# A hybrid decoder layer on one core: first norm, state-gate blocks, split heads and last norms reordered

## The chip, the cores and the metric

One core of a Trainium2 chip runs the whole program. Its engines work side by side, each from its own in-order queue: TensorE (PE: matmuls, with weight loads shown apart as PEld), VectorE (DVE), ScalarE (ACT), GpSimd (POOL) and SyncE (SP, which issues DMAs; ACT and POOL can issue DMAs too). An engine stops at an instruction whose semaphore has not come. The metric is the device time of one execution in microseconds (us).

## The reference

```python
xn = rmsnorm(h, norm1_g)                     # h: 16 meta tokens and 512 tokens, 1024 channels
u_s, x_m, z_m, g_s, g_m = split(xn @ w_in)
y_s = s5_branch(u_s, ...) @ w_ssm_out        # diagonal SSM scan, gelu, y * sigmoid(y @ w_glu)
y_m = mlstm_branch(x_m, z_m, ...) @ w_ml_out # conv, silu, gates, 4 heads of matrix memory
mixed = sigmoid(g_s) * y_s + sigmoid(g_m) * y_m
h = h + mixed @ w_out
h = h + peer_ffn(rmsnorm(h, norm2_g), ...)   # top 16 of 16384 one-neuron experts, 8 heads
return rmsnorm(h, final_norm_g)[:, 16:]
```

Everything is float32, and the norms divide by the root of the mean square of a token's 1024 channels.

## The kernel before

Each float32 matmul is done as three fast ones: an operand x is split into a rounded half `x_h` (made on ACT) and the rest `x_l` (made on DVE or POOL, as x minus `x_h`), and `mm3` issues high x high, high x low and low x high. Weights come in blocks of 128x1024: `wblock` loads one over SP's queue and splits it, the low half on POOL for some block numbers. A scheduler sets the order of the instructions on each engine from the order in which the code is written and from its own times; `later`, `behind` and `keep_in_program_order` add constraints. Four tiles (`pmm`) and four more (`ptr`) of PSUM take the products.

The stages, in the order of PE's work:

- **First norm and u.** x comes transposed, in pieces `xr0`, `xr1` (eight blocks k of 128 channels). ACT writes `xnh` = x times the norm's scale `g1` (L246), DVE the rest `xnl` (L247). The root of the mean square (`sqt`, `ssp`, `n1...`, `nt`) is applied behind the products.
- **SSM, conv and state gates.** The SSM's input blocks (`wx0` to `wx7`) give `xm`; DVE drains each half into `xmt` (L181) and runs a causal convolution into `xct` (three steps each, L443), followed by a sigmoid on ACT (L446). State-gate blocks `gs0` to `gs7` (L82, L85, L86; weights `wgs`) stand between them; 24 matmuls each. The scan's output `ys` (copied by ACT at L579) is turned round through DRAM: eight writes `yd` (L586), eight reads `yt` (L588), then gelu into `yg` (L661) and its split `ygh`, `ygl`.
- **Forget and input gates.** `gate` (64 matmuls with the zero-padded weights `wgt`) is copied with a bias into `rwa` (L606) and turned by `xtp`, `lip` and later `lfp`; log-sigmoid and two scans of DVE follow.
- **glu, so, heads.** `glu` and `so` finish the SSM branch. Four heads follow; each ends by writing its two blocks of `xct`. When all are done, the eight blocks are split into `ymh`, `yml` and `mo0` to `mo7` multiply them.
- **wo and q.** `wo` gives h (tiles `x0`, `x12`, `x3q`); for each of four token tiles the second norm makes `xn`, PE transposes it (`x2t`) and it is split into `x2h`, `x2l`; the queries `q0`, `q1` read these, half of the tokens at a time.
- **Experts.** The scores, the choice of experts, hidden products (`h`) and a loop over 128 keys j: `w` and `v` are split and `o0`, `o1`, `o2` collect the products of token tiles 1 to 3; tile 0 is summed by DVE in `ac0`. The last keys' products run tile by tile.
- **Last norm.** For each token tile in turn: two adds into `hr` (L1482), squares on ACT, two multiplications by the final scale (`sq`, L1484), a chain of ten small DVE operations for 1/root, and two scalings and two DMAs out.

Of the kernel before, what the change touches and what calls it, by code (L numbers as in the profile page):

```python
# [126 lines left out]
def front(tc, a, dbg, cst, dram, xnp, ident, h2d, gds, x0, qt01, dump, split, mm3, rsqrt, rsqrt_cols):  # L127
# [3 lines left out]
    with es:  # L131
# [58 lines left out]
        xr = [half(f"xr{j}", f"x{'cm'[j]}t0") for j in range(2)]  # L190
        g1 = small("g1", (P, NK), a["par"][:, :NK])
        wu = [None] * 4
        for k in range(0, NK, 2):
            (SY, A)[k // 2 % 2].dma_start(xr[k // 4][:, k % 4:k % 4 + 2], a["xt"][k // 2])
            if k == 0:
                wu[0] = wblock(a["w_in"][0], "wu0")
        wu[1] = wblock(a["w_in"][1], "wu1")

# [358 lines left out]
        for b, n in ((0, 0), (8, 2)):  # L557
            V.tensor_copy(wgt[:, b:b + 8, :2 * H], wgs[:, n])

# [160 lines left out]
        V.tensor_copy(cb[:, 14:18], cbp[:, 14:18])  # L720
        p5.close()
        pm_ = ExitStack()
        phase["pool"] = pm_.enter_context(tc.tile_pool(name="pmh", bufs=2, reuse_waits="tile"))
        phase["q"] = pm_.enter_context(tc.tile_pool(name="pmq", bufs=12, reuse_waits="tile"))
        zs_ = {}
# [71 lines left out]
        pms, squares = {}, []  # L797

        def weights(h):

            mup = phase["q"].tile([P, S], F32, tag="mu", name=f"mu{h}", bufs=2)
            SY.dma_start(mup, mud[h:h + 1].to_broadcast([P, S]))
# [16 lines left out]
        for h in range(H):  # L819
# [62 lines left out]
        phase["pool"] = es.enter_context(tc.tile_pool(name="pe", bufs=1, reuse_waits="tile"))  # L882
        ymh = [half(f"ymh{j}", f"pA{j}", (P, 4, S), F32R) for j in range(2)]
        yml = [half(f"yml{j}", f"pB{j}", (P, 4, S), F32R) for j in range(2)]
# [35 lines left out]
        g2, ss2 = None, []  # L920
        for c, slots in ((0, ("xct0", "xct1", "mix0", "xmt0")), (1, ("pA0", "pA1", "pB0", "pB1"))):
            wo = wout(c, slots)
            if c == 1:
# [4 lines left out]
                wq = [wblock(a["w_q"][s_], f"wq{s_}") for s_ in range(2)]  # L928
                qp = []
            for i in range(NT):  # L930
                p = pmm(f"wo{i}{c}")
# [13 lines left out]
                if i == 1:  # L945
                    xn12, xn3 = half("xn12", "xct0", (P, 2, D)), half("xn3", "xct1", (P, 2, D))
                xn = (xn12[:, 0], xn12[:, 1], xn3[:, 0])[i - 1] if i else x0
                V.scalar_tensor_tensor(xn, xs[i], rstd, g2, op0=OP.mult, op1=OP.mult)
                for j in range(2):
                    p = ptr(f"x2t{i}{j}", (P, 4, P))  # L950
                    for k in range(4):
                        PE.transpose(p[:, k], xn[:, (4 * j + k) * P:(4 * j + k + 1) * P], ident)
                    split(xh[j][:, :, i * P:(i + 1) * P], xl[j][:, :, i * P:(i + 1) * P], p)

        for t in (slice(0, S // 2), slice(S // 2, S)):
            for s_ in range(2):
                if t.start == 0:
                    qp.append(pmm(f"q{s_}"))
                proj(*wq[s_], qp[s_][:, t], lambda k: [x[k // 4][:, k % 4, t] for x in (xh, xl)])
                A.copy(qt01[:, s_, t], qp[s_][:, t])  # L960
        if dbg is not None and "h2" in dbg:
# [4 lines left out]
def peer(tc, a, out, dbg, cst, dram, xh, xl, blanks, ident, h2d, gds, x0, qt01, dump, split, mm3, rsqrt_cols):  # L966
# [20 lines left out]
    with es:  # L987
# [420 lines left out]
        def products(i, j, wh, wl, vh, vl, pin=None, halves=(0, 1)):  # L1408
# [4 lines left out]
            return last  # L1413

        due = 0
        loop[0] = True
        for j in range(NKEY):
# [23 lines left out]
            for last in (0, 1):  # L1441
# [116 lines left out]
```

## Time and profile before

| | |
|---|---|
| median of 3 runs | 1695.78 us (1695.61 to 1697.59) |
| profiled execution | 1696.09 us, its span 1694.4 us |
| PE / PEld busy | 97% / 86% of the span |
| DVE / ACT / POOL busy | 76% / 41% / 42% |
| mean granted TensorE clock | 0.993 of 2.4 GHz |

The span runs from the first to the last instruction; the time holds 1.7 us more around it. PE is busy nearly throughout, so what can be won lies in the few places where PE stands still, runs at a lower clock, or has not begun or has ended. The page cuts the span into 40 slices of 42 us; the first and the last of them are those with PE at 7 and 6 tenths, all others at 9.

### The profile page before, as it was taken

What the parts mean: (1) busy time and instruction counts of PE and PEld (TensorE: products, weight loads), DVE (VectorE), ACT (ScalarE), POOL (GpSimd) and SP (SyncE); (2) the same over time, 40 slices, a digit from 0 to 9 for tenths busy, and PEclk for the clock granted to TensorE, in tenths of its full rate; (3) what the DMA queues carried; (4) which work ended last, traced back from release to release, by engine and by line L of the source; (5) the groups of instructions that cost most, each with busy time, mean ns of one, the idle gap of its engine ahead of it and who ended that gap; (6) DMA issues with size and microseconds to landing.
All of it is one profiled execution on the core that took longest, in us unless ns stands there. A gap on an engine that the chain in (4) does not pass through costs nothing.

```text
span 1694.4 us, 25464 instructions
## 1 busy us (share of the span) xinstructions
PE 1650.4 (97%) x9387; PEld 1461.3 (86%) x9387; DVE 1279.9 (76%) x2599; ACT 690.6 (41%) x1021; POOL 709.3 (42%) x476
## 2 busy tenths in 40 slices
PE   7999999999999999999999999999999999999996
PEld 6888688777888899999999988888888888888885
DVE  6995642266478899977884598878878897888876
ACT  4543545432332334556664433333333333333323
POOL 2011022223122378888886043333335564554520
PEclk9999999999999999999999999999999999999998
DMA  5514254212452347699999999999998999999963
GB/s 184 119 51 100 63 199 153 70 40 75 173 199 87 112 91 183 155 271 299 297 300 337 350 380 400 337 345 360 350 362 318 363 391 368 362 371 349 335 245 129
DMA packets 173364, 409.83 MB, mean 242 GB/s; under 512 B 44468, under 2 KB 89652, under 8 KB 172088
## 3 DMA queue, kind: packets, MB, share of 16 engines
q1 hardware_dynamic: 113624, 266.51, 45.4%
q0 software_dynamic: 55328, 134.31, 23.3%
q10 hardware_dynamic: 4288, 7.39, 1.3%
q8 instruction: 73, 1.20, 0.3%
q14 instruction: 51, 0.42, 0.1%
HBM read 360.86 MB, written 47.29 MB: 241 GB/s over the span
## 4 chain that ended last, share of the span: by engine, by line
PE 84%; DVE 8%; DMA 4%; ACT 2%; issue 2%; POOL 0%; SPq 0%; ACTq 0%; DVEq 0%; POOLq 0%
PE h L82 10%; PE h L85 10%; PE h L86 10%; PE o L82 10%; PE o L86 10%; PE o L85 10%; PE gp L1333 2%; PE q L86 2%; PE q L85 2%; PE q L82 2%; DMA wo<-in_w_out 1%; PE s L839 1%; PE n L848 1%; PE gm L346 1%; PE gm L349 1%
## 5 line engine op out<-in xcount | busy, mean ns | idle before, releaser
L82 PE MATMUL h<-x2h,uh 128*128 128x384 f32 x1024 | 345.5, 337 | 0.2 <-ACT act L1024 0.2
L85 PE MATMUL h<-x2l,uh 128*128 128x384 f32 x1024 | 343.5, 335 | 0.0
L86 PE MATMUL h<-x2h,ul 128*128 128x384 f32 x1024 | 343.2, 335 | 0.0
L85 PE MATMUL o<-vl,wh 128*128 128x512 f32 x768 | 280.1, 391 | 0.8 <-DVE vl L79 0.8
L82 PE MATMUL o<-vh,wh 128*128 128x512 f32 x768 | 280.3, 391 | 0.2 <-ACT wh L1435 0.2
L1043 POOL DMA_INDIRECT g<-in_v,e x128 | 200.2, 1564 | 187.7 <-DVE ac L1058 169.1
L86 PE MATMUL o<-vh,wl 128*128 128x512 f32 x768 | 266.5, 390 | 0.5 <-DVE wl L1450 0.5
L1267 POOL DMA_INDIRECT gds<-gw,ix x128 | 239.7, 1872 | 46.3 <-issue 36.9
L1043 POOL DMA_INDIRECT g<-in_u,e x103 | 115.6, 1122 | 217.3 <-DVE jk L1050 214.3
L79 DVE TENSOR_TENSOR vl<-v,vh 128x1024 fp32r<-128x1024 f32 x128 | 156.2, 1220 | 63.5 <-ACT vh L78 63.3
L79 DVE TENSOR_TENSOR ul<-u,uh 128x1024 fp32r<-128x1024 f32 x128 | 156.1, 1219 | 56.1 <-ACT uh L78 45.4
L78 ACT ACTIVATE uh<-u 128x1024 fp32r<-128x1024 f32 x128 | 135.4, 1058 | 152.6 <-PE h L85 119.8
L82 PEld LDWEIGHTS h<-x2h,uh 128*128 128x128 f32 x1024 | 192.3, 188 | 4.1 <-ACT act L1024 0.5
L85 PEld LDWEIGHTS h<-x2l,uh 128*128 128x128 f32 x1024 | 192.3, 188 | 1.9
L86 PEld LDWEIGHTS h<-x2h,ul 128*128 128x128 f32 x1024 | 192.3, 188 | 1.8
L78 ACT ACTIVATE vh<-v 128x1024 fp32r<-128x1024 f32 x128 | 134.6, 1055 | 103.3 <-issue 73.0
L86 PEld LDWEIGHTS o<-vh,wl 128*128 128x128 f32 x768 | 144.2, 188 | 31.4 <-DVE wl L1450 1.2
L85 PEld LDWEIGHTS o<-vl,wh 128*128 128x128 f32 x768 | 144.1, 188 | 30.2 <-DVE vl L79 1.1
L82 PEld LDWEIGHTS o<-vh,wh 128*128 128x128 f32 x768 | 143.7, 188 | 27.6 <-ACT wh L1435 0.5
L1058 DVE SCALAR_TENSOR_TENSOR ac<-g,w,ac 128x1024 f32<-128x1024 f32 x127 | 162.4, 1279 | 0.0
L1024 ACT ACTIVATE act<-h 128x384 f32<-128x384 f32 x128 | 61.6, 481 | 224.3 <-PE h L86 224.2
L1050 DVE SCALAR_TENSOR_TENSOR jk<-g,x 128x1024 bf16<-128x1024 f32 x103 | 125.5, 1219 | 0.0
(535 smaller groups left out, 2930.1 us busy)
## 6 DMA issues: line engine op xcount, KB each, us to landing
u<-in_ut SPq DMA_DIRECT2D x128, 512.0 KB
v<-in_v SPq DMA_DIRECT2D x128, 512.0 KB
gd<-stg SPq DMA_DIRECT2D x8, 2048.0 KB
gi<-gd SPq DMA_DIRECT2D x16, 1024.0 KB
ad<-act SPq DMA_DIRECT2D x80, 192.0 KB
acl<-ad SPq DMA_DIRECT2D x80, 192.0 KB
gds<-qt SPq DMA_DIRECT2D x8, 1024.0 KB
gi<-gds SPq DMA_DIRECT2D x16, 512.0 KB
```

The source lines that it names most:

```text
L78: A.activation(hi, src, AF.Copy)
L79: return eng.tensor_tensor(lo, src, f32(hi), op=OP.subtract)
L82: i_ = PE.matmul(ps, lh, rh, start=first, stop=False)
L85: PE.matmul(ps, lh, rl, start=False, stop=False)
L86: return PE.matmul(ps, ll, rh, start=False, stop=last)
L346: i_ = PE.matmul(ps_, hi[:, k], rh, start=k == 0, stop=False)
L1024: A.activation(acts[j], p, AF.Gelu_apprx_tanh)
L1043: return GP.indirect_dma_start(out=t, out_offset=None, in_=a["u"] if s_ < P else a["v"], in_offset=bass.IndirectOffsetOnAxis(ap=e0[:, c:c ...
L1050: i_ = V.scalar_tensor_tensor(jk, g, 1.0, x0, op0=OP.mult, op1=OP.mult, accum_out=hsl[:, c:c + 1])
L1058: i_ = V.scalar_tensor_tensor(ac0, g, w0[:, c:c + 1], ac0, op0=OP.mult, op1=OP.add)
L1267: i_ = GP.indirect_dma_start(out=gds.rearrange("b i j t -> (b i j t)").unsqueeze(1), out_offset=bass.IndirectOffsetOnAxis(ap=ix[:, c:c + 1 ...
L1333: PE.matmul(p[:, t], o1[:, a_, :, b_], ow[:, n, a_, :, b_], start=n == 0, stop=n == 1)
```

## The change

1. **Start.** `g1`'s DMA goes from POOL's queue to ACT's, ahead of x. The blocks `wu0`, `wu1` are still loaded first, but split only among the pieces of x, after k = 1 and k = 7; k = 2 of x stands behind the high half of `wu0`.
2. **Gate weights.** The two copies into `wgt` go from DVE to ACT, and a memset of `rwa` from DVE to POOL.
3. **State gates.** `gs5` is computed before `gate`; the block of `gs7` is split ahead of gelu; four of the eight `yd` writes go on ACT's queue.
4. **Heads.** Blocks 0 to 3 (heads 0 and 1) are split at the end of their head, into a pool of their own; one buffer less for the head's quarter tiles and for `mu`. Some slots of `wo` change places.
5. **Second norm.** The transposes of token tiles 2 and 3 stand between the four query products.
6. **Last norm.** Tile 0 is added, squared and scaled inside the key loop; tiles 1 and 2 share one chain and are scaled by ACT; tile 3 is alone. `gf` and `hr` are loaded earlier.

```diff
-            i_ = split(hi[:, :nk], lo[:, :nk], raw[:, :nk], GP if ... else V)
+            h_ = A.activation(hi[:, :nk], raw[:, :nk], AF.Copy)
+            if on is not None:
+                highs.append(later(h_, on))
+            i_ = tt(lo[:, :nk], raw[:, :nk], f32(hi[:, :nk]), OP.subtract, GP if ... else V)
...
-        g1 = small("g1", (P, NK), a["par"][:, :NK])
+        g1 = small("g1", (P, NK), a["par"][:, :NK], A)
...
             xhs = A.activation(h_, x_, AF.Copy, scale=g1[:, k:k + 1])
+            if k == 2:
+                later(xhs, highs[0])
             V.scalar_tensor_tensor(l_, x_, g1[:, k:k + 1], f32(h_), op0=OP.mult, op1=OP.subtract)
+            if k == 1 or k == NK - 1:
+                n = k // 2 and 1
+                wu[n] = wblock(a["w_in"][n], f"wu{n}", raw=wu[n], on=xhs)
...
-            V.tensor_copy(wgt[:, b:b + 8, :2 * H], wgs[:, n])
+            A.copy(wgt[:, b:b + 8, :2 * H], wgs[:, n])
...
-        gsgate(4)
-        wg56 = [wblock(a["w_in"][20 + b], f"wgs{b}") for b in (5, 6)]
+        for b in (4, 5):
+            gsgate(b)
+        wg6 = wblock(a["w_in"][26], "wgs6")
...
-            SY.dma_start(yd[t_].rearrange("g c n -> c g n"), ys[t_ * CH:(t_ + 1) * CH])
+            (SY, A)[t_ % 2].dma_start(yd[t_].rearrange("g c n -> c g n"), ys[t_ * CH:(t_ + 1) * CH])
...
-        V.memset(rst, 1.0)
+        GP.memset(rst, 1.0)
...
-        for b in range(5, NK):
-            gsgate(b, wg56.pop(0) if wg56 else None)
+        gsgate(6, wg6)
+        gsgate(7)
...
+                if b < 4:
+                    ysplit(b)
...
-        for b in range(NK):
-            split(ymh[b // 4][:, b % 4], yml[b // 4][:, b % 4], xct[b // 4][:, b % 4, NM:])
+        for b in range(4, NK):
+            ysplit(b)
...
+                waiting.append((i, xn))
+                if i < 2:
+                    turned_(*waiting.pop())
+            if c:
+                for s_ in range(2):
+                    query(s_, 0)
+                    turned_(*waiting.pop(0))
+                for s_ in range(2):
+                    query(s_, 1)
...
+            if j in (NKEY - 4, NKEY - 3):
+                if sq[0] is None:
+                    sq[0] = up.tile([P, D], F32, tag="ulo", name="sq30", bufs=3)
+                added(0, (j - (NKEY - 4),))
+            elif j == NKEY - 2:
+                scaled((0,))
...
-        for i in range(NT):
-            ss = fin.tile([P, 2], F32, name=f"ss3{i}")
...
+        for i in range(1, NT):
+            added(i)
+            if i == 2:
+                scaled((1, 2))
+        scaled((3,))
```

`added(i, halves)` holds, for each half of a tile's columns, the add on DVE, the square on ACT and the multiplication by the final scale on DVE; `scaled(of)` one chain for all tiles in `of` and their scalings and DMAs, with ACT scaling both halves of tiles 1 and 2.

**ACT, gate weights.** ACT's queue around the block `wx6`, before:

```order
L547 COPY l2t1_1135<-l2p6_1180 112x16x16
L547 COPY l2t0_1134<-l2p7_1187 128x16x16
L547 COPY l2t1_1135<-l2p7_1187 128x16x16
L78 ACTIVATE wx6_h_1346<-wx6_w_1344 128x1024
L437 ACTIVATE xct1_1215<-xmt1_1214,par_107 128x528
```

and of the change:

```order
L562 COPY l2t1_1135<-l2p6_1180 112x16x16
L562 COPY l2t0_1134<-l2p7_1187 128x16x16
L562 COPY l2t1_1135<-l2p7_1187 128x16x16
L573 COPY wgt_1472<-wgs_517 128x8x8 x2
L170 ACTIVATE wx6_h_1346<-wx6_w_1344 128x1024
L452 ACTIVATE xct1_1215<-xmt1_1214,par_99 128x528
```

The two copies into `wgt` now stand ahead of the high half of `wx6`; the low half on POOL needs that high half.

**ACT, behind the scan's output.** From the last copies of `ys` to the weights of `glu`, before:

```order
L579 COPY ys_1477<-y10_1530 128x8x64
L579 COPY ys_1477<-y11_1531 128x8x64
L78 ACTIVATE wgs6_h_1624<-wgs6_w_1622 128x1024
L489 ACTIVATE mix1_1582<-mix1_1582 128x512
L606 ACTIVATE rwa_1646<-gate0_1648,bif_109 128x264
L606 ACTIVATE rwa_1646<-gate1_1649,bif_109 128x264
L661 ACT_TABLE_LOAD
L661 ACTIVATE yg_1825<-yt_1629 128x2048
L78 ACTIVATE ygh_1827<-yg_1825 128x512 x4
L620 COPY rwa_1646<-lip0_1684 4x264
```

and of the change:

```order
L602 DMA yd_1655<-ys_1477 16x32x64 x4
L170 ACTIVATE wgs6_h_1651<-wgs6_w_1649 128x1024
L504 ACTIVATE mix1_1582<-mix1_1582 128x512
L170 ACTIVATE wgs7_h_1794<-wgs7_w_1792 128x1024
L677 ACT_TABLE_LOAD
L677 ACTIVATE yg_1825<-yt_1656 128x2048
L504 ACT_TABLE_LOAD
L504 ACTIVATE mix1_1582<-mix1_1582 128x512
L78 ACTIVATE ygh_1827<-yg_1825 128x512 x4
L622 ACTIVATE rwa_1673<-gate0_1675,bif_101 128x264
L622 ACTIVATE rwa_1673<-gate1_1676,bif_101 128x264
```

The high half of `wgs7` came behind all of the first list, and is now ahead of gelu. The two copies into `rwa` have gone from ahead of gelu to behind gelu, a second table load, a sigmoid of `mix` and the four `ygh`.

**PE, first products behind the heads.** Behind the last head's transposes (`ht31`), before:

```order
L873 MATMUL ht31_3473<-ident_60,hs3_3347 128x128 x3
L346 MATMUL mo0_3515<-ymh0_3485,wmo0_h_3511 128x512
L346 MATMUL mo1_3550<-ymh0_3485,wmo1_h_3546 128x512
L348 MATMUL mo0_3515<-yml0_3487,wmo0_h_3511 128x512
L349 MATMUL mo0_3515<-ymh0_3485,wmo0_l_3512 128x512
L346 MATMUL mo0_3515<-ymh0_3485,wmo0_h_3511 128x512
```

and of the change:

```order
L364 MATMUL mo0_3518<-ymh0_2212,wmo0_l_3515 128x512
L361 MATMUL mo1_3553<-ymh0_2212,wmo1_h_3549 128x512
L363 MATMUL mo1_3553<-yml0_2213,wmo1_h_3549 128x512
L361 MATMUL mo0_3518<-ymh1_3498,wmo0_h_3514 128x512
L363 MATMUL mo0_3518<-yml1_3499,wmo0_h_3514 128x512
L364 MATMUL mo0_3518<-ymh1_3498,wmo0_l_3515 128x512
```

The first of these is the twelfth matmul of `mo0` behind the transposes; all twelve read the early halves `ymh0`, `yml0`, and two of `mo1` follow. Before, `mo1` began behind the first matmul of `mo0`.

## Rows read from the trace of the kernel before

**Rows 1.** From the profile page: busy time of PE with its share of the span, the weight loads, DVE, ACT and POOL.

```profile
PE 1650.4 (97%) x9387; PEld 1461.3 (86%) x9387; DVE 1279.9 (76%) x2599; ACT 690.6 (41%) x1021; POOL 709.3 (42%) x476
```

**Rows 2.** The waits of PE over the whole span: the waiting operation and its line, the releaser, us in all, times, the longest.

```profile
PE u L346 <- ACT wu_h L78: 11.2, 1, 11.2
PE xm L346 <- DVE xmt L181: 2.2, 1, 2.2
PE x2t L952 <- DVE xn L948: 2.0, 1, 2.0
PE mo L348 <- DVE yml L79: 1.2, 1, 1.2
PE mo L346 <- ACT ymh L78: 1.1, 1, 1.1
PE so L346 <- DVE mix L181: 0.9, 3, 0.4
PE o L85 <- DVE vl L79: 0.8, 1, 0.8
```

**Rows 3.** Four stretches of the span: busy us of each engine (with its instructions), PEclk (the granted TensorE clock, 1.00 being 2.4 GHz), DMA share, GB/s.

```profile
130.00:140.00 10.00, 10.00 (x69) 9.93 (x70) 10.00 (x14) 3.11 (x4) 1.83 (x1) 0.75 0.34 107
170.00:180.00 10.00, 7.83 (x27) 5.53 (x26) 7.35 (x23) 8.82 (x15) 0.00 (x0) 0.83 0.17 38
380.00:390.00 10.00, 9.09 (x33) 7.29 (x34) 5.07 (x8) 2.55 (x5) 0.31 (x1) 0.83 0.18 52
470.00:480.00 10.00, 7.96 (x53) 6.99 (x52) 8.80 (x20) 3.50 (x8) 0.00 (x0) 1.00 0.50 189
```

**Rows 4.** The timeline of ACT at the start (columns of every timeline here: start us, busy us, engine, line, operation, out<-in, count, and in brackets the idle time before and its releaser).

```profile
7.57 2.61 ACT L246 ACTIVATE xnh<-xr,g 128x528 fp32r<-128x528 f32 x4 [2.83 <-DMA g<-in_par]
```

**Rows 5.** The timeline at 113 to 130 us, of ACT, then POOL, then DVE.

```profile
113.03 1.06 ACT L78 ACTIVATE wx_h<-wx_w 128x1024 fp32r<-128x1024 f32 x1 [1.60 <-issue]
...
115.90 2.88 POOL L79 TENSOR_TENSOR wx_l<-wx_w,wx_h 128x1024 fp32r<-128x1024 f32 x1
...
117.00 1.93 DVE L558 COPY wgt<-wgs 128x64 f32<-128x64 f32 x2
...
121.94 4.84 DVE L443 SCALAR_TENSOR_TENSOR xct<-xmt,par,xct 128x527 f32<-128x527 f32 x7
126.69 0.44 DVE L181 TENSOR_TENSOR xmt<-xm,nt 128x264 f32<-128x264 f32 x1
```

**Rows 6.** The timeline at 151 to 178 us, of SP's DMA queue, then ACT.

```profile
152.08 7.63 SPq L586 DMA_DIRECT2D yd<-ys  x8
159.81 4.92 SPq L588 DMA_DIRECT2D yt<-yd  x8
...
151.00 1.06 ACT L579 COPY ys<-y 128x512 f32<-128x512 f32 x2
...
159.96 0.93 ACT L606 ACTIVATE rwa<-gate,bif 128x264 f32<-128x264 f32 x2 [1.88 <-PE gate L599]
167.31 1.28 ACT L661 ACT_TABLE_LOAD   x1 [6.42 <-DMA yt<-yd]
168.60 1.92 ACT L661 ACTIVATE yg<-yt 128x2048 f32<-128x2048 f32 x1
170.55 2.20 ACT L78 ACTIVATE ygh<-yg 128x512 fp32r<-128x512 f32 x4
...
177.21 0.63 ACT L489 ACTIVATE mix<-mix 128x512 f32<-128x512 f32 x1
```

**Rows 7.** Two stretches: while the packets of yd move, and while those of yt move (columns as in rows 3).

```profile
153.00:162.00 9.00, 9.00 (x87) 6.04 (x86) 0.69 (x1) 2.50 (x4) 2.38 (x1) 1.00 0.68 127
162.00:167.00 5.00, 5.00 (x28) 3.71 (x27) 0.00 (x0) 0.00 (x0) 0.00 (x0) 1.00 1.01 205
```

**Rows 8.** PE at 150 to 184.5 us: two groups by line (operation, shapes, count | busy us, mean ns), then, of the timeline, the first matmul behind its wait.

```profile
L617 PE MATMUL xtp<-sel,rwa 128*128 128x4 f32 x10 | 1.2, 244 | 0.0
L619 PE MATMUL lip<-rwa,sel 128*4 128x264 f32 x4 | 1.1, 386 | 0.0
...
175.95 0.79 PE L82 MATMUL gs<-xnh,wgs_h 128*128 128x512 f32 x1 [2.05 <-ACT wgs_h L78]
```

**Rows 9.** The timeline at 372 to 385 us: PE (18 matmuls of gm from the first row to the second, one after the other), then DVE.

```profile
372.66 0.39 PE L346 MATMUL gm<-xnh,wgm_h 128*128 128x512 f32 x1
...
376.60 0.40 PE L349 MATMUL gm<-xnh,wgm_l 128*128 128x512 f32 x1
...
378.96 6.11 DVE L79 TENSOR_TENSOR yml<-xct,ymh 128x512 fp32r<-128x512 f32 x8
```

**Rows 10.** The timeline of DVE at 477 us.

```profile
477.07 1.28 DVE L79 TENSOR_TENSOR x2l<-x2t,x2h 128x512 fp32r<-128x512 f32 x2
```

**Rows 11.** The timeline of the end: PE's last matmul, then DVE, then ACT's DMA queue.

```profile
1679.85 0.39 PE L86 MATMUL o<-vh,wl 128*128 128x512 f32 x1
...
1684.96 0.68 DVE L1482 TENSOR_TENSOR hr<-o,hr 128x512 f32<-128x512 f32 x1
1687.82 0.16 DVE L105 SCALAR_TENSOR_TENSOR n33e<-ss 128x1 f32<-128x1 f32 x1
...
1689.75 0.49 DVE L1491 TENSOR_SCALAR hr<-sq,n33o 128x512 f32<-128x512 f32 x1
...
1690.56 0.34 ACTq L1492 DMA_DIRECT2D out<-hr  x1
```

More of the change, by code (lines that the diff above doesn't have):

```diff
@@ L195, in front @@
             if k == 0:
-                wu[0] = wblock(a["w_in"][0], "wu0")
-        wu[1] = wblock(a["w_in"][1], "wu1")
+                wu[0] = wload(a["w_in"][0], "wu0")
+        wu[1] = wload(a["w_in"][1], "wu1")
         par = sm.tile([P, sum(n for _, n in PAR)], F32, name="par")
@@ L721, in front @@
         p5.close()
+        yhp = es.enter_context(tc.tile_pool(name="yhp", bufs=1))
+        ymh, yml = ([yhp.tile([P, 4, S], F32R, name=f"ym{x}0"), None] for x in "hl")
         pm_ = ExitStack()
         phase["pool"] = pm_.enter_context(tc.tile_pool(name="pmh", bufs=2, reuse_waits="tile"))
-        phase["q"] = pm_.enter_context(tc.tile_pool(name="pmq", bufs=12, reuse_waits="tile"))
+        phase["q"] = pm_.enter_context(tc.tile_pool(name="pmq", bufs=11, reuse_waits="tile"))
         zs_ = {}
@@ L797, in front, with ysplit @@
         pms, squares = {}, []
+        def ysplit(b):
+            split(ymh[b // 4][:, b % 4], yml[b // 4][:, b % 4], xct[b // 4][:, b % 4, NM:])
         def weights(h):
-            mup = phase["q"].tile([P, S], F32, tag="mu", name=f"mu{h}", bufs=2)
+            mup = phase["q"].tile([P, S], F32, tag="mu", name=f"mu{h}", bufs=1)
             SY.dma_start(mup, mud[h:h + 1].to_broadcast([P, S]))
@@ L882, in front @@
         phase["pool"] = es.enter_context(tc.tile_pool(name="pe", bufs=1, reuse_waits="tile"))
-        ymh = [half(f"ymh{j}", f"pA{j}", (P, 4, S), F32R) for j in range(2)]
-        yml = [half(f"yml{j}", f"pB{j}", (P, 4, S), F32R) for j in range(2)]
-        for b in range(NK):
-            split(ymh[b // 4][:, b % 4], yml[b // 4][:, b % 4], xct[b // 4][:, b % 4, NM:])
+        ymh[1], yml[1] = (half(f"ym{x}1", s_, (P, 4, S), F32R) for x, s_ in (("h", "pA0"), ("l", "pB1")))
+        for b in range(4, NK):
+            ysplit(b)
         mxh = [half(f"mxh{j}", f"pC{j}", (P, 4, S), F32R) for j in range(2)]
@@ L929, in front, with turned_, query @@
                 qp = []
+            def turned_(i, xn):
+                first = None
+                for j in range(2):
+                    p = ptr(f"x2t{i}{j}", (P, 4, P))
+                    for k in range(4):
+                        i_ = PE.transpose(p[:, k], xn[:, (4 * j + k) * P:(4 * j + k + 1) * P], ident)
+                        if i > 1 and not first:
+                            tc.keep_in_program_order(i_)
+                        first = first or i_
+                    split(xh[j][:, :, i * P:(i + 1) * P], xl[j][:, :, i * P:(i + 1) * P], p)
+            def query(s_, n):
+                t = slice(n * S // 2, (n + 1) * S // 2)
+                if n == 0:
+                    qp.append(pmm(f"q{s_}"))
+                proj(*wq[s_], qp[s_][:, t], lambda k: [x[k // 4][:, k % 4, t] for x in (xh, xl)])
+                A.copy(qt01[:, s_, t], qp[s_][:, t])
+            waiting = []
             for i in range(NT):
@@ L945, in front @@
                 if i == 1:
-                    xn12, xn3 = half("xn12", "xct0", (P, 2, D)), half("xn3", "xct1", (P, 2, D))
+                    xn12, xn3 = half("xn12", "pA1", (P, 2, D)), half("xn3", "pB0", (P, 2, D))
                 xn = (xn12[:, 0], xn12[:, 1], xn3[:, 0])[i - 1] if i else x0
                 V.scalar_tensor_tensor(xn, xs[i], rstd, g2, op0=OP.mult, op1=OP.mult)
[L949 to L960, printed above, removed]
+                waiting.append((i, xn))
[7 more added lines that the diff above has]
+                    query(s_, 1)
         if dbg is not None and "h2" in dbg:
@@ L1413, in products, with added, scaled @@
             return last
+        fin = es.enter_context(tc.tile_pool(name="fin", bufs=1, reuse_waits="tile"))
+        gf = qt01.rearrange("p a s -> p (a s)")
+        hr, sq = [None] * NT, [None] * NT
+        cc = [slice(c * 512, (c + 1) * 512) for c in range(2)]
+        jq = fin.tile([P, D // 2], BF16, name="jq")
+        ss = fin.tile([P, 2, NT], F32, name="ss3")
+        def added(i, halves=(0, 1)):
+            y, x = hr[i], op_[i - 1] if i else ac0
+            if sq[i] is None:
+                sq[i] = up.tile([P, D], F32, tag="vraw", name=f"sq3{i}", bufs=4)
+            for c in halves:
+                inorder(V.tensor_tensor(y[:, cc[c]], x[:, cc[c]], y[:, cc[c]], op=OP.add))
+                A.activation(jq, y[:, cc[c]], AF.Square, scale=1.0 / math.sqrt(D), accum_out=ss[:, c, i:i + 1])
+                inorder(V.tensor_tensor(sq[i][:, cc[c]], y[:, cc[c]], gf[:, cc[c]], op=OP.mult))
+        def scaled(of):
+            n = len(of)
+            rstd = rsqrt_cols(fin, ss[:, 0, of[0]:of[0] + n], n, f"n3{of[0]}", more=ss[:, 1, of[0]:of[0] + n])
+            for i in of:
+                for c in range(2):
+                    o, x, rs = hr[i][:, cc[c]], sq[i][:, cc[c]], rstd[:, i - of[0]:i - of[0] + 1]
+                    if c or i in (1, 2):
+                        A.activation(o, x, AF.Copy, scale=rs)
+                    else:
+                        V.tensor_scalar(o, x, rs, None, op0=OP.mult)
+                    (SY, A)[c].dma_start(out[i * P:(i + 1) * P, cc[c]], o)
         due = 0
```

42 lines of the change are left out of this document (14 added, 28 removed).

## Prediction

> **What bounds the kernel now.** I read the page first: PE is busy for 1650.4 us, 97% of the span [rows 1]. The list of PE's waits then says where it is not: 11.2 us before its first matmul, and a handful of stalls of 1 to 2 us [rows 2]. The stretches of 10 us add what a stall can cost behind itself: the granted clock is 0.83 at 170 to 180 and at 380 to 390 and 0.75 at 130 to 140, each time beside stalls of PE, but 1.00 at 470 to 480, which holds a wait of 2.0 us too [rows 3]. So a stall of some 2 us is followed by a stretch at the lower of the two levels (1.2 instead of 2.4 GHz) or not; 10 x (1 - 0.83) = 1.7 us is its price where it comes. Last comes the tail: PE's last matmul starts at 1679.85, ACT's last DMA at 1690.56 [rows 11]. All that PE does between is unchanged in number, so I cost the change by start, stalls, clock and tail. The profiled execution took 1696.09 us against a median of 1695.78; the sum is made on the former.
>
> **1. Start.** ACT begins its splits of x at 7.57, released by `g1`'s DMA [rows 4]. With `g1` on ACT's own queue this wait shrinks, and `wu0_h` no longer stands behind all four pieces of `xnh0`, so PE should start some 2 us earlier. It then meets the piece k = 2, whose low half is made late, and stands again. I count 1.0 us gained, between 0 (the pieces of x or `wu0` land too late for more) and 2.0.
>
> **2. Gate weights.** POOL's split `wx_l` runs from 115.90 for 2.88 us, and two tiny copies on DVE take 1.93 us beside it [rows 5]: the two block each other. The copies go to ACT, ahead of `wx6_h`, which moves from 113.03 to about 116.4, as they must wait for POOL's memset; POOL's split moves behind it and then holds up DVE's next operations instead. DVE so gains nothing here, and a convolution step more (4.84 / 7 = 0.69 us [rows 5]) stands ahead of the drain `xmt` at 126.69. I take +0.5 for DVE's convolutions. PE's stall of 2.2 us there becomes two of 1 to 1.5, probably without the clock's fall. That gain is not counted, since PE then waits at the next place for a chain that starts on DVE.
>
> **3. State gates.** Before, the last block of `gs` starts at 175.95 behind a wait of 2.05 us for ACT's `wgs_h` [rows 8]. One matmul takes (376.60 - 372.66) / 17 = 0.232 us [rows 9], 24 of them 5.6; with 1.7 for the clock the block is done at 183.2. After, `wgs7_h` is early, but `xtp` and `lip` wait for `rwa`, which now stands behind gelu on ACT [rows 6]. The chain: the last copies of `ys` end at 152.06; -1.0 from the start, +0.5 from DVE, and two copies of 0.53 more that now stand behind the last sigmoid, +1.1, give 152.6. From `ys` to gelu's table load it took 152.06 to 167.31, 15.25 us [rows 6]. SP issued `yd` for 7.63 us while the DMA engines were 0.68 busy; for `yt` they were at 1.01 [rows 7]. With two queues issuing, the 9 us of `yd` could fill the engines, 9 x (1 - 0.68) = 2.9 less; by issue alone half of 7.63, 3.8 less; if the engines take small packets no faster, 0. I take 2.7: the table load starts at 165.2. Table load and gelu take 167.31 to 170.55, 3.2; then a second table load and `mix`, 1.28 + 0.63; `ygh`, 2.2; `rwa`, 0.9 [rows 6]: 173.4. PE gets there at 169 to 171 (173.9 before, less 2.3 for `xtp` and `lip` and 1.0 for the start, perhaps less 2 more for the clock), so it stands for 2.5 to 4.5 us and I count the fall of the clock: `xtp` and `lip` 2.3 [rows 8], the other 22 matmuls 5.1, 1.7 for the clock: 182.5. That is 0.7 less than 183.2, the start's 1.0 included; a stall has moved more than gone. The bounds: no gain by the second queue, +2.0; engines filled and no fall of the clock, -3.6.
>
> ScalarE: Activation LUTs of the Trainium skill, What ACT_TABLE_LOAD costs, gives a switch 2.66 us, of which 1.38 are a drain. The row has gelu start 1.29 us behind the start of its load, so this trace does not agree; by the page the two loads in this chain would make the sum 2.8 us worse.
>
> **4. so.** PE waits 0.9 us there for DVE's `mix` [rows 2]; `wso4_l` comes earlier in DVE's queue. -0.5, between 0 and -0.9.
>
> **5. Heads split early.** Behind the heads PE waits 1.1 for `ymh` and 1.2 for `yml` [rows 2], and the clock falls to 0.83 [rows 3]. DVE needs 6.11 us for the eight low halves [rows 9]. After, twelve matmuls of `mo0` and two of `mo1` have their operands ready: 14 x 0.232 = 3.2 us of work, in which ACT and DVE finish the next block's split (0.53 and 0.76 us each). Both waits and the clock's loss go: 1.1 + 1.2 + 1.7 = 4.0; `mo0` also ends four matmuls sooner, which lets later weights in, 0.5 of the possible 0.9. -4.5, between -2.3 (the clock falls anyway) and -5.0. The early splits cost eight small operations on ACT and DVE; I give them no price, as no head operation stands among the waits that are priced here, and if the heads have no room for them they cost 0.53 to 0.76 us each.
>
> **6. Transposes.** PE waited 2.0 us for `xn` of tile 2. It now goes on into `q0`, but that needs `x2l` of tile 1, which DVE starts only at 477.07, behind that same `xn`; half of 1.28 us [rows 10] later PE goes on, less 0.2 for issue: +0.4. The clock did not fall behind the 2.0 [rows 3]; if it falls now, +2.1.
>
> **7. Last norms.** DVE's fourth block starts at 1684.96 and its chain ends at 1689.75 [rows 11]; each block takes 5.2 us and four stand in line. After, tile 0 lies in the key loop, under PE's products. PE's last group begins some 0.4 later, since `wh` of the last key stands behind tile 0's scaling on ACT, so PE ends at 1680.6 and `o1` at 1676.4. DVE adds and multiplies tile 2's second half to 1677.8, and its chain of 1.95 (1687.82 to 1689.75) ends at 1679.8. Tile 3's halves follow, to 1682.6; ACT meanwhile does four scalings, then tile 3's squares, to 1684.8. Chain 1.95, scaling 0.8: the last DMA starts at 1687.5 instead of 1690.56, -3.0, between -2.0 and -3.6.
>
> **Sum.** -0.7 - 0.5 - 4.5 + 0.4 - 3.0 = -8.3, and 1696.1 - 8.3 = 1687.8 us. PE shows no idle time worth a row in the key stages, so nothing there swallows a shift.
>
> **The rivals.**
> *The second queue buys nothing*, 0.20. If the engines take `yd`'s small pieces no faster from two queues, `rwa` is 2.7 us later: 1690.5. For it: the engines were 0.68 busy, not idle. Against: for `yt` they reached 1.01. In DMA: Bandwidth & Descriptors of the Trainium skill, Issuing engines are not separate DMA queues, it says that issuing from several engines saves only the sequencer's time; by that rule too what may be saved is SP's 7.63 us of issue.
> *All stalls short*, 0.20. `yd` gains 3.8, 1.1 more than counted, and PE's clock stays up behind `xtp`, 1.7 more: 1685.0. The wait at 470 us without a fall speaks for it, that of 175.95 against it.
> *The tail gains nothing*, 0.08. If tile 0's work in the loop holds the last keys' `wh` and `vl`, PE's last group begins late by as much as the tail saves, 3.0: 1690.8. PE already waits 0.8 for `vl` there.
> *Slower than before*, 0.04. The `xtp` chain alone: if `yd` and `yt`, now on two rings, get in each other's way and land later than 173.5 instead of 165.2, the 8.3 are gone; at the whole `yd` stretch of 9 us done twice PE's stall would grow by 11.7 (2.7 not won and 9 more), 1699.5. The share of 0.68 says that the engines are not overfull, so this is unlikely.
> *The forecast* has the other 0.48.
>
> **How the numbers follow.** The bounds of the forecast's own terms, taken not all at one end, give some 3.5 us to either side, 1684.3 to 1691.3. The range reaches to the short-stall case below and to the two at 1691 above, with a margin for the clock behind the queries (+1.7): 1683.0 to 1692.5. A run can tell 0.2%, 3.4 us. Faster by more than that (below 1692.4) are the forecast, the short stalls and most of the two that end near 1691; I leave 0.09 of those and of the forecast's upper end for within 0.2%: 0.87, 0.09, 0.04.
>
> **What would show it.** PE's waits: no `wgs_h`, `ymh` or `yml`; a new one of 2.5 to 4.5 us at `xtp` for `rwa`, one of 2.4 at the queries for `x2l`, two of about 1 us at `xm`. Clock 1.00 at 380 to 390. Gelu's table load at 165; the last DMA 7 us behind PE's last matmul instead of 10.5. I am wrong if gelu starts at 167.5 or later, if PE does not wait at `xtp` at all, or if new waits stand in the heads, whose pools lose a buffer.

## The result

The changed kernel takes 1686.67 us (median of 5 runs, 1685.49 to 1689.44) against 1695.78 us (5 runs, 1694.83 to 1697.59): a ratio of 0.9948, 95% interval 0.9934 to 0.9963. That is 9.1 us less, where 8.3 were forecast. The profiled executions stand at 1686.67 and 1696.09, and the accounts below are made between these two.

The profile page gives PE 2.7 us less busy time than in [rows 1], in a span 9.4 us shorter.

```profile
PE 1647.7 (98%) x9387; PEld 1459.8 (87%) x9387; DVE 1276.8 (76%) x2584; ACT 693.7 (41%) x1026; POOL 707.6 (42%) x476
```

The list of PE's waits after (columns as in [rows 2]). The waits for `ymh`, `yml` and the `xn` of tile 2 are gone, and so is the one for `wgs_h` of [rows 8]. New are 4.7 us at `xtp`, 1.8 at `q` for `x2l`, two of 1 us at `xm` and 1.3 at `o` for `wh`. The 1.1 at `l1p` stood before as well; [rows 2] leaves it out, and a wait of 1.5 at `v` for `vm` that stood before and is not in this list.

```profile
PE u L361 <- ACT wu_h L170: 9.6, 1, 9.6
PE xtp L633 <- ACT rwa L622: 4.7, 1, 4.7
PE q L363 <- DVE x2l L79: 2.0, 2, 1.8
PE o L82 <- ACT wh L1505: 1.5, 2, 1.3
PE l1p L470 <- DVE w1r L191: 1.1, 1, 1.1
PE xm L361 <- DVE xmt L191: 1.1, 1, 1.1
PE xm L364 <- POOL wx_l L191: 1.0, 1, 1.0
```

The stretches of [rows 3], after. The clock is 1.00 at 130 to 140 and 380 to 390, where it was 0.75 and 0.83; at 170 to 180 it is 0.66, lower than before.

```profile
130.00:140.00 10.00, 10.00 (x118) 9.93 (x117) 10.00 (x14) 2.96 (x4) 2.15 (x1) 1.00 0.30 107
170.00:180.00 10.00, 6.25 (x19) 4.36 (x20) 4.72 (x9) 7.88 (x15) 0.00 (x0) 0.66 0.14 53
380.00:390.00 10.00, 9.50 (x41) 7.29 (x40) 4.97 (x8) 2.75 (x3) 3.02 (x2) 1.00 0.17 52
```

The timelines of SP's queue, ACT and PE at 150 to 176 us, after, which answer to [rows 6, 8]: `yd` goes out on two queues, the gelu's table load starts 1.2 us sooner than before, and `rwa`, now behind it, holds PE.

```profile
152.83 4.21 SPq L602 DMA_DIRECT2D yd<-ys  x4
157.15 6.35 SPq L604 DMA_DIRECT2D yt<-yd  x8
...
150.78 2.03 ACT L594 COPY ys<-y 128x512 f32<-128x512 f32 x4
152.84 4.31 ACTq L602 DMA_DIRECT2D yd<-ys  x4
...
166.11 1.28 ACT L677 ACT_TABLE_LOAD   x1 [6.13 <-DMA yt<-yd]
167.40 1.92 ACT L677 ACTIVATE yg<-yt 128x2048 f32<-128x2048 f32 x1
169.33 1.28 ACT L504 ACT_TABLE_LOAD   x1
170.63 0.63 ACT L504 ACTIVATE mix<-mix 128x512 f32<-128x512 f32 x1
171.16 2.17 ACT L78 ACTIVATE ygh<-yg 128x512 fp32r<-128x512 f32 x4
173.24 0.83 ACT L622 ACTIVATE rwa<-gate,bif 128x264 f32<-128x264 f32 x2
...
173.75 2.29 PE L633 MATMUL xtp<-sel,rwa 128*128 128x4 f32 x10 [4.71 <-ACT rwa L622]
```

The timeline of the end, which answers to [rows 11]: PE's last matmul, DVE's last chain, ACT. The last DMA stands 7.89 us behind PE's last matmul; before it was 10.71.

```profile
1673.50 0.39 PE L86 MATMUL o<-vh,wl 128*128 128x512 f32 x1
...
1678.65 0.16 DVE L105 SCALAR_TENSOR_TENSOR n33e<-ss 128x1 f32<-128x1 f32 x1 [1.33 <-ACT jq L1470]
...
1674.69 1.95 ACT L1480 ACTIVATE hr<-sq,n31o 128x512 f32<-128x512 f32 x3 [2.01 <-DVE n31o L99]
...
1681.39 0.34 ACTq L1483 DMA_DIRECT2D out<-hr  x1
```

Where the time went, from the start of the same matmul in both traces (after less before, us; the step is what the stage adds):

| start of | after less before | step |
|---|---|---|
| the first of u (PE begins) | -1.55 | -1.6 |
| the first of l1p | 0.00 | +1.6 |
| the last of y | -3.1 | -3.1 |
| the first of so (behind xtp and glu) | +0.5 | +3.6 |
| the first of z | -0.5 | -1.0 |
| the last of gm (the heads) | -0.8 | -0.3 |
| the first of wo (behind most of mo) | -6.0 | -5.2 |
| the first of sc (behind x2t and q) | -6.5 | -0.5 |
| PE's last | -6.35 | +0.1 |
| last output DMA | -9.17 | -2.8 |

Up to `so` nothing is gained. The step with the heads' split gives 5.2 and the end 2.8. PE's first matmul at 9.63 is the earliest of all runs with this start; the seven others have it at 10.0 to 10.1, 1.1 ahead of before.

### The profile page after: what moved, and what is told of

Its sections match the earlier page's. It is cut to its first block, busy times and chain, and to the rows that moved or that the text cites. A ratio compares the mean times of both kernels' runs of the same rounds, so it can differ in the third digit from the quotient of the medians.

```text
span 1685.0 us, 25453 instructions
## 1 busy us (share of the span) xinstructions
PE 1647.7 (98%) x9387; PEld 1459.8 (87%) x9387; DVE 1276.8 (76%) x2584; ACT 693.7 (41%) x1026; POOL 707.6 (42%) x476
## 4 chain that ended last, share of the span: by engine, by line
PE 85%; DVE 7%; DMA 3%; ACT 2%; issue 1%; SPq 1%; POOL 0%; ACTq 0%; DVEq 0%; POOLq 0%
PE h L82 10%; PE h L86 10%; PE h L85 10%; PE o L86 10%; PE o L82 10%; PE o L85 10%; PE gp L1374 2%; PE q L85 2%; PE q L86 2%; PE q L82 2%; DMA wo<-in_w_out 1%; PE s L861 1%; PE n L870 1%; PE gm L361 1%; PE gm L364 1%
## 5 line engine op out<-in xcount | busy, mean ns | idle before, releaser
L79 DVE TENSOR_TENSOR vl<-v,vh 128x1024 fp32r<-128x1024 f32 x128 | 156.0, 1219 | 58.8 <-ACT vh L78 58.7
L79 DVE TENSOR_TENSOR ul<-u,uh 128x1024 fp32r<-128x1024 f32 x128 | 155.9, 1218 | 56.4 <-ACT uh L78 49.0
```

What stands on the lines that cost most here:

```text
L79: return eng.tensor_tensor(lo, src, f32(hi), op=OP.subtract)
```

## The experiments

Experiments 2 and 8 were timed in rounds; the others ran once with a profile, and are read stage by stage.

**1. The old start.** Before's first loads, norm scale and weight splits in the changed kernel.

```
-g1 = small("g1", (P, NK), a["par"][:, :NK], A)
+g1 = small("g1", (P, NK), a["par"][:, :NK])
...
-        wu[0] = wload(a["w_in"][0], "wu0")
-wu[1] = wload(a["w_in"][1], "wu1")
+        wu[0] = wblock(a["w_in"][0], "wu0")
+wu[1] = wblock(a["w_in"][1], "wu1")
...
```

> The changed kernel with the start of the kernel before (g1 on POOL's queue, wu0 and wu1 split as they were); all else as changed. In the trace of the changed kernel PE's first matmul is 1.55 us earlier than before, the block xm starts 0.72 us earlier, but l1p starts at 72.87 us in both, behind the same wait of 1.1 us for DVE's w1r. Theory: the start's gain is swallowed there, by a chain on ACT that waits for the landing of the block wgs1 (ACT goes on at 54.76 us in both traces). Then this kernel has xm 0.7 us later than the changed one, l1p within 0.1 us of 72.87, and its time is that of the changed kernel within 0.3 us in every later stage. Rival: the start's gain is carried on through DVE's queue as was forecast; then l1p, the end of the convolutions and the first glu matmul are all 0.7 to 1.0 us later than in the changed kernel.

Measured: 1685.38 us, 1.3 less than the changed kernel's profiled run and 0.1 less than the fastest of its five. PE begins 1.72 later than there, `l1p` 0.91 later and the gates 2.45 later (the clock fell in `xm`). At `xtp` PE then stands for less, and the clock at 170 to 180 is 0.83 instead of 0.66:

```profile
174.12 1.38 PE L628 MATMUL xtp<-sel,rwa 128*128 128x4 f32 x10 [2.62 <-ACT rwa L617]
```

```profile
170.00:180.00 10.00, 7.38 (x30) 4.82 (x29) 5.21 (x11) 8.24 (x15) 0.00 (x0) 0.83 0.16 53
```

`glu` starts 0.93 sooner than in the changed kernel: the same 36 matmuls from `xtp` to `glu` take 8.93 us here and 10.23 there. So the start's gain isn't eaten at `l1p`, as the theory had it (the equal times there came from a weight load that landed 0.45 us quicker in the execution of before); as in the rival, the convolutions end 0.95 later here. But `ys` ends at 152.79, against 152.81 in the changed kernel. The order on ACT is not the same: here two of the four copies of `ys` stand ahead of the last sigmoid, there all four stand behind it. The rows of this run, then the last sigmoid of the changed kernel:

```profile
150.23 1.06 ACT L589 COPY ys<-y 128x512 f32<-128x512 f32 x2
151.17 0.66 ACT L456 ACTIVATE qt<-xct 128x528 f32<-128x528 f32 x1
151.72 1.07 ACT L589 COPY ys<-y 128x512 f32<-128x512 f32 x2
```

```profile
150.23 0.65 ACT L461 ACTIVATE qt<-xct 128x528 f32<-128x528 f32 x1 [0.78 <-DVE xct L191]
```

PE goes on at `xtp` only 0.37 later. What the start would be worth there with the order on ACT left as it was, this run does not show; the 1.3 us that it is ahead come from the 36 matmuls behind the wait.

**2. The gelu behind `rwa`.** One line: gelu waits for the copies that write `rwa`, so they run first.

```
-A.activation(yg, yt..., AF.Gelu_apprx_tanh)
+later(A.activation(yg, yt..., AF.Gelu_apprx_tanh), biased)
```

> The changed kernel with one more constraint: gelu on ACT stands behind the two copies into rwa (and so behind gate), nothing left out. Theory: the wait of 4.7 us at xtp is due only to the place of the two rwa copies on ACT behind gelu, the second table load, mix and ygh; ACT is idle for 6.1 us ahead of gelu, so the copies cost nothing there. PE then does not wait at xtp, its clock stays at 1.00 at 170 to 180 us, and glu starts at 176 to 177 us instead of 184.0: the time falls by 6 to 7.5 us, to about 1679.5. Rival: glu is bound by the ACT chain from gelu to ygh, wglu and by DVE's low halves; then PE waits at glu instead, glu starts at 178 to 180 and the gain is 4 to 6 us. Second rival: the wait moves on to so or to the heads, and less than 3 us remain.

Measured: 1681.41 us (4 runs, 1680.18 to 1682.08), a ratio to before's runs of the same rounds of 0.9906 (0.9889 to 0.9922). ACT writes `rwa` in time in which it stood idle, PE does not stop, and the clock stays at 1.00:

```profile
163.97 0.93 ACT L622 ACTIVATE rwa<-gate,bif 128x264 f32<-128x264 f32 x2 [1.93 <-PE gate L615]
166.08 1.28 ACT L677 ACT_TABLE_LOAD   x1 [1.18 <-DMA yt<-yd]
...
168.81 1.17 PE L633 MATMUL xtp<-sel,rwa 128*128 128x4 f32 x10
```

```profile
170.00:180.00 10.00, 10.00 (x43) 7.57 (x43) 7.80 (x23) 8.13 (x13) 0.00 (x0) 1.00 0.15 55
```

`glu` starts at 177.75 instead of 183.98, 6.2 sooner; the end keeps 5.5 of it. What is lost stands in `so`, which takes 24.96 us up to the first of `z` where the changed kernel took 24.16. A wait of 1.46 for `vm` appears at `v`, but it costs nothing: from the first of `z` to the last of `gm` both kernels take 156.0. The copies into `rwa` stood behind the gelu only because the order of instructions on ACT said so; nothing that they read comes from it.

**3. `yd` from one queue.**

```
-(SY, A)[t_ % 2].dma_start(yd[t_].rearrange("g c n -> c g n"), ...)
+SY.dma_start(yd[t_].rearrange("g c n -> c g n"), ...)
```

> The changed kernel with all eight writes yd on SP's queue, as before the change; nothing else. In the changed kernel the time from the last copy of ys (152.8 us) to gelu's table load (166.1) is 13.3 us against 15.25 before. Theory: the second queue is what shortened it, since SP's issue of one write after another was the pace; then the table load comes at about 168.1 here, xtp's wait grows from 4.7 to about 6.7 us and everything behind is 2.0 us later: about 1688.7. Rival (by the rule that issuing from several engines saves next to nothing): the two queues share the same 16 engines, and what shortened it is something else (other traffic at that time); then the table load stays within 0.4 us of 166.1 and the time within 0.5 us.

Measured: 1691.13 us, of which 2.4 are a lower clock at 25 to 30 us, in code that is the same. From the end of `ys` (153.20 + 2.03) to the table load it takes 15.23, as before (15.25), against 13.30 with two queues: between these two runs the second queue is worth 1.93 us, and PE's wait at `xtp` grows by 1.9. The seven other runs with two queues take 12.87 to 14.32, so it is worth 0.9 to 2.4. The 36 matmuls behind it take 10.90.

```profile
155.26 7.43 SPq L602 DMA_DIRECT2D yd<-ys  x8
...
170.46 1.28 ACT L677 ACT_TABLE_LOAD   x1 [8.04 <-DMA yt<-yd]
...
178.10 2.30 PE L633 MATMUL xtp<-sel,rwa 128*128 128x4 f32 x10 [6.61 <-ACT rwa L622]
```

**4. The heads split behind the loop**, all eight together, with the old buffers.

```
-                if b < 4:
-                    ysplit(b)
...
-for b in range(4, NK):
+for b in range(NK):
     ysplit(b)
```

> The changed kernel without the early split of the blocks of heads 0 and 1: no pool of their own, all eight blocks split behind the heads, with the pool sizes and slots of the kernel before. Theory: the early split is worth what the stage mo gained, 5.2 us (1.1 and 1.2 us of waits, 1.7 us of the clock, 0.7 us of the wait for wmo_l and some 0.5 more): the heads end within 0.3 us of the changed kernel's 377.1, mo starts 1 us behind them, PE's clock falls at 380 to 390 us, and all behind is 4.5 to 5.5 us later: about 1692. Rival: mo0's matmuls, put one after the other, are what pays, and without the early split only the first wait of about 1 us comes back, since the clock need not fall: 1 to 2.5 us later, about 1688.5.

Measured: 1695.7 us, with the clock lower at 25 to 30 us (+2.0 to 2.3) and behind the queries (+1.9). The stage of `mo` alone, from the last of `gm` to the first of `wo`, is 5.26 longer, of which 2.9 are waits. Both waits and the clock's fall are back:

```profile
380.46 0.73 PE L361 MATMUL mo<-ymh,wmo_h 128*128 128x512 f32 x2 [1.09 <-ACT ymh L78]
...
382.40 0.56 PE L363 MATMUL mo<-yml,wmo_h 128*128 128x512 f32 x1 [1.21 <-DVE yml L79]
```

```profile
380.00:390.00 10.00, 8.33 (x28) 6.40 (x29) 6.56 (x9) 4.05 (x8) 1.80 (x1) 0.83 0.16 52
```

**5. The old last norms**, four row tiles in line behind the key loop.

```
-            if j in (NKEY - 4, NKEY - 3):
-                added(0, (j - (NKEY - 4),))
-            elif j == NKEY - 2:
-                scaled((0,))
...
-for i in range(1, NT):
-    added(i)
-    if i == 2:
-        scaled((1, 2))
-scaled((3,))
+for i in range(NT):        # add, square, chain, scale, as before
```

> The changed kernel with the last norms as the kernel before has them: all four row tiles behind the key loop, each with a chain of its own. Theory (my term of 3.0 us, of which the traces of before and after show 2.8): the last output DMA is issued 10.3 to 10.7 us behind TensorE's last matmul instead of 7.5, and TensorE itself ends .3 to .6 us earlier, because its wait for wh near the end is .77 again instead of 1.35; together 2.2 to 2.9 us later than the changed kernel, about 1689.2 us where the rest runs as in its profile. Rival (the tail gains nothing, the rest came from TensorE): the last DMA stays 7.5 to 8.5 us behind TensorE's end.

Measured: 1691.22 us; PE is 2.45 later at `l1p`, behind the clock's fall at 25 to 30 us, and 1.61 at its last matmul. From it to the last DMA it takes 10.69, as before, and PE's wait for `wh` (1.35) is again one of 0.76 for `vl`. The tail is worth 2.8 us behind PE's last matmul; PE pays 0.6 of wait for it. From the first of `sc` to the last DMA, with both in it, it is worth 2.4.

```profile
1675.11 0.39 PE L86 MATMUL o<-vh,wl 128*128 128x512 f32 x1
...
1685.80 0.34 ACTq L1533 DMA_DIRECT2D out<-hr  x1
```

**6. The old order of transposes and queries.**

```
-                if i < 2:
-                    turned_(*waiting.pop())
+                turned_(*waiting.pop())
...
-                for s_ in range(2):
-                    query(s_, 0)
-                    turned_(*waiting.pop(0))
-                for s_ in range(2):
-                    query(s_, 1)
+                for n in range(2):
+                    for s_ in range(2):
+                        query(s_, n)
```

> The changed kernel with the transposes of x2 and the halves of q in the order of the kernel before: all four tiles turned, then q in four pieces. Theory (I forecast that the new order costs .4 us; the traces of before and after show it .5 us better): the stage from the first matmul of q or x2t to the first of sc is .2 to .6 us longer, with a wait of about 2.0 us at x2t or q and one of .5 at x. Rival, my forecast: the stage is .4 us shorter. If the two are within .2 us, the order of the transposes is worth nothing here.

Measured: 1686.21 us. From the first of `wo` to the first of `sc` it takes 67.77 us here and 68.09 in the changed kernel, but 67.65 to 68.09 in all six profiles of this change with the new order and without a fall of the clock there (the changed kernel, experiments 1, 2, 3, 5 and 7). So the theory fell, and the 0.4 of my forecast is not shown either: these runs can tell no worth of the order. PE waits 1.59 at the transposes here and 1.82 at `q` in the changed kernel:

```profile
470.61 1.06 PE L959 MATMUL x2t<-ident,xn 128*128 128x128 f32 x8 [1.59 <-DVE xn L990]
```

```profile
470.77 0.39 PE L363 MATMUL q<-x2l,wq_h 128*128 128x256 f32 x1 [1.82 <-DVE x2l L79]
```

The wait of 0.51 for `x` that stood in this stage before is absent in both, so it went with another part of the change; which one, I did not isolate.

**7. The `wgt` copies and the fill of `rwa` on DVE.**

```
-            A.copy(wgt[:, b:b + 8, :2 * H], wgs[:, n])
+            V.tensor_copy(wgt[:, b:b + 8, :2 * H], wgs[:, n])
-        GP.memset(rst, 1.0)
+        V.memset(rst, 1.0)
```

> The changed kernel with the two copies of wgt and the fill of rwa on VectorE again, as in the kernel before. Theory: within xm (113 to 130 us) TensorE has one wait of about 2.2 us in the place of two of 1.0, so the stage from xm's first to the gates' first matmul is .1 to .4 us longer, .7 more if the granted clock falls behind the wait; TensorE still meets rwa at 173.7 to 174.3 us, as it waits there for ys, the DMAs and the gelu, not for itself, and its wait at xtp becomes shorter by what it came later: the span stays within .5 us. Rival: these copies set the end of the convolutions and so of the state gates; then rwa is written .4 us or more later and the span is longer by as much.

Measured: 1686.82 us, 0.15 from the changed kernel. One wait of 2.17 stands in `xm` in place of 0.97 and 1.05, and the clock falls behind it (0.95 and 0.88 in the two stretches of 10 us from 120):

```profile
126.92 0.39 PE L361 MATMUL xm<-xnh,wx_h 128*128 128x264 f32 x1 [2.17 <-DVE xmt L191]
```

PE is then 1.23 late at `gate`, and its wait at `xtp` is 3.8 instead of 4.7. The copies of `ys` start at 150.76, against 150.78, though DVE was 0.26 ahead of the changed kernel at 111 us: from there to the end of the convolutions it takes 0.24 longer than in the changed kernel, as in the kernel before (0.23). So the move of these copies to ACT gave DVE 0.2.

**8. Five more orders on top of experiment 2.** Each is one added dependence that only orders instructions.

```
gs block 0:  later(sigmoid, last sine)
wgt copies:  later(copy, last product of x)
head 0:      later(mask on mu, last values of head 1)
x2, tile 2:  later(xn, split of tile 1)
last norms:  added(0) at NKEY - 5, NKEY - 4; scaled((0,)) at NKEY - 3
```

> The kernel with the gelu behind rwa (1681.4 us), with five more orders: the first state gate's sigmoid behind the last sine (two table loads less ahead of w1r), the wgt copies behind the last product of x, the masks on mu of head 0 behind the values of two heads, the norm of x2's tile 2 behind the split of tile 1, and the first last-norm tile one key block earlier. Each is aimed at one wait of TensorE: 1.1 us at l1p for w1r, 1.0 at xm for POOL's wx_l, 1.5 at v for vm, 1.6 at q for x2l, .6 of the 1.3 at o for wh. If TensorE is the bound from there to the end and each wait goes without a new one, 1681.4 - 5.0 = 1676 us (1675 to 1678.5). Rival: the waits move on, since VectorE and ScalarE are late by the same amount in the next piece: 1680 to 1682. Waits named differently but as long would say the rival; the state gates' chain has some 4 us in hand at xtp and 6 at glu, so they should not bind.

Measured: 1681.18 us (4 runs, 1680.26 to 1683.09), a ratio to before's runs of the same rounds of 0.9915 (0.9892 to 0.9938): no different from experiment 2. The aimed waits of `l1p`, `wx_l`, `v`, `x2l` and `wh` are gone or down to 0.2, and PE's list has others in their place:

```profile
PE xm L361 <- DVE xmt L191: 2.3, 2, 1.6
PE x2t L963 <- DVE xn L998: 1.0, 1, 1.0
```

PE is 1.5 us ahead of experiment 2 at `l1p` and 2.0 at the first of `y`; by the last of `y` it is 0.2 behind. In `xm` the waits merge into 0.63 and 1.63 close together, with a lower clock behind them. DVE, which drains that stage, is busy for all of the 10 us below in both kernels; that this is why the waits only moved is argued, not shown. Stretches of experiment 2, then of this kernel:

```profile
125.00:130.00 5.00, 3.94 (x32) 3.80 (x31) 5.00 (x9) 1.77 (x2) 0.73 (x1) 0.93 0.00 0
130.00:135.00 5.00, 5.00 (x33) 5.00 (x32) 5.00 (x6) 0.65 (x1) 2.09 (x1) 0.73 0.61 206
...
228.00:232.00 4.00, 4.00 (x57) 3.48 (x47) 2.34 (x15) 0.50 (x2) 2.09 (x2) 1.00 0.93 343
232.00:236.00 4.00, 2.54 (x32) 2.03 (x32) 3.13 (x11) 3.25 (x7) 0.62 (x1) 1.00 0.74 266
```

```profile
125.00:130.00 5.00, 3.95 (x19) 3.95 (x20) 5.00 (x6) 1.77 (x2) 2.12 (x1) 0.62 0.10 13
130.00:135.00 5.00, 5.00 (x32) 5.00 (x32) 5.00 (x8) 0.64 (x1) 0.69 (x1) 0.70 0.56 200
...
228.00:232.00 4.00, 4.00 (x32) 3.72 (x32) 2.10 (x14) 0.71 (x2) 1.69 (x1) 0.57 0.92 332
232.00:236.00 4.00, 4.00 (x57) 3.39 (x56) 3.33 (x9) 3.01 (x6) 1.23 (x2) 1.00 0.78 287
```

In `xm` the clock costs 5 x (0.38 + 0.30) = 3.4 us here and 1.7 there. At `v` the wait of 1.46 has become four us at 0.57, 1.7 us; but the wait is also missing, beside a low clock, in the changed kernel and in experiments 1, 4 and 7, which have no such order. At `q` the 1.40 became 0.98 and 0.07 was won. Only the end keeps its share: the last DMA starts 0.95 sooner.

## Why the prediction was right, and where it was not

The forecast of 1687.8 lies 1.1 us from the median. Its terms were these.

**Start, gate weights, state gates: -0.7 forecast, +0.5 measured.** The mechanism was the forecast one: a wait of 2.5 to 4.5 us was expected at `xtp`, and 4.71 came. It was a near thing: gelu starts at 167.40, and a start at 167.5 or later was named as a sign of being wrong. Its sizes were off. The second queue saves 1.93 us (experiment 3), not 2.7, and `ys` ends at 152.81, not 152.6, so the table load starts at 166.1, not 165.2. Of that 0.9 us, 0.35 reached PE, which resumes at 173.75 instead of 173.4. And from there to `glu` it took 10.23 us, not 9.1. Experiment 2 ran this stretch at 1.00 with seven matmuls of `gs` more: 8.94 - 7 x 0.232 = 7.3 us, about the 7.4 that I had counted, so the clock's fall cost 2.9, not 1.7. I had taken its price from waits of about 2 us in [rows 3], but the length of the wait does not set it: worked out in the same way it is 1.6 behind the 2.62 of experiment 1 and 3.2 behind the 2.65 of experiment 5, 2.5 behind the 4.88 of experiment 4 and 3.6 behind the 6.61 of experiment 3. The row of experiment 5, whose `glu` starts at 186.25:

```profile
175.72 1.96 PE L633 MATMUL xtp<-sel,rwa 128*128 128x4 f32 x10 [2.65 <-ACT rwa L622]
```

That `ys` ended within 0.2 us of the forecast was luck: the 1.0 of the start did not reach `l1p` in this pair of traces, and the 0.5 that I charged DVE for POOL's split was wrong in sign, since DVE gained 0.2 (experiment 7). The gelu's activation again starts 1.29 us behind the start of its table load, and the next 1.30; ScalarE: Activation LUTs of the Trainium skill, What ACT_TABLE_LOAD costs, would have made each 2.66, and the measurement decides.

**so: -0.5 forecast, -1.0 measured**, not tested apart. The earlier `wso4_l` alone does not explain it: in experiments 2 and 8, where PE does not stand at `xtp` and comes to `so` 6 us sooner, the stage takes 24.96 and 24.93 again, against 25.13 before and 24.16 in the changed kernel. So most of this gain seems to go with PE's late arrival.

**Heads: -4.5 forecast, -5.2 measured, -5.26 by experiment 4.** The two waits and the clock make 4.0, as counted; the 0.5 for later weights came as the wait of 0.66 for `wmo_l` that is gone, and 0.6 is not broken down. The eight early splits cost the heads nothing that shows: from the first of `z` to the last of `gm` they take 155.97 us, against 156.26 before and 156.27 in experiment 4. The wait of 1.5 for `vm` of the kernel before does not stand in the changed kernel, where the clock is at 0.50 at 235 to 237 instead; experiments 2, 3, 5 and 6 have that wait and a clock of 1.00, and take 156.0 too.

**Transposes: +0.4 forecast, -0.5 between the two traces.** Experiment 6 shows no cost of the new order. The stage is shorter than before because the wait for `x` is gone and PE stands for 1.82 at `x2l` where it stood for 2.04 at `xn`; 2.4 were forecast at `x2l`.

**Last norms: -3.0 forecast for the whole end; -2.7 between the two traces from the first of `sc` on, -2.4 by experiment 5.** Behind PE's last matmul it is -2.8 in both, down to 7.89 us, where some 7 were forecast. PE's wait there is 0.6 longer, for `wh`, where 0.4 was forecast.

Of the rivals, the second queue that buys nothing fell with experiment 3. The rule of DMA: Bandwidth & Descriptors of the Trainium skill, Issuing engines are not separate DMA queues, by which issuing from several engines saves only the sequencer's time, fits the size: the issue took 7.43 us on one queue and 4.31 on two, and of these 3.1 us 1.93 were won. The tail that gains nothing fell with experiment 5, and neither the slower case nor the short stalls came, since PE did wait and the clock did fall. The misses, +1.2 up to `so` and -0.5 to -1.0 each at `so`, the heads and the transposes, went against each other; that the total is better than its parts is luck.

## What to carry to other kernels

A wait that ends a chain through another engine swallows most of what PE gains or loses ahead of it (in experiment 7 PE came to the gates 1.23 us later and went on at `xtp` 0.34 later): look for such a wait first, and for what stands ahead of its releaser on that engine for no reason of data. Here one line of order on ACT, the short copies into `rwa` ahead of the gelu, took 5.3 us off the median, as much as the best part of the whole change. Don't take the clock's loss from the length of the wait ahead of it: behind two waits of 2.6 us it was 1.6 and 3.2 us. And where another engine is busy without a gap, don't expect that a removed wait is won.

## What was not expected of the hardware

- The same code is followed by the lower clock in one execution and not in another. At 25 to 30 us, where PE is busy throughout behind 20 small matmuls, the granted clock was 0.66 in experiments 3 and 5, 0.73 in 4 and 1.00 in the changed kernel and experiments 1, 2, 6, 7 and 8; it costs 2.2 to 2.5 us up to `l1p`. Behind the two waits of 1 us in `xm` it was 1.00 (at 130 to 140) in the changed kernel and experiments 3, 4 and 6, and 0.83 to 0.86 in experiments 1, 2 and 5, which took 1.6 us more from `l1p` to the last of `y`.
- The clock fell without a wait: to 0.50 or 0.51 over two us behind the small transposes and matmuls of `cbp` and `vm`, with PE busy throughout, in the changed kernel and experiments 1, 4, 7 and 8. In the kernel before and in experiments 2, 3, 5 and 6 the same work ran at 1.00 and then met a wait of 1.4 to 1.5 for `vm`. From the first of `z` to the last of `gm` it took 155.9 to 156.3 us in all ten, so neither the wait nor the fall decides the length of that stage.
- A split on POOL goes with a slower DVE beside it: the addition into `rt` took 3.10 us beside POOL's `wx_l` of 2.59 and 1.25 alone. In [rows 5] it was the two tiny copies that took 1.93 beside such a split; no run has them on DVE alone.
